# A Fourier stage's second step: table halves stand, data moves, and transposes turn the result

## The chip, the cores and the metric

The kernel runs on one NeuronCore of one Trainium2 chip. The metric is device microseconds for one execution of the whole program. Engines are named as in the profile: PE (TensorE products), PEld (its weight loads), DVE (VectorE), ACT (ScalarE), POOL (GpSimd), SP (SyncE, which issues nearly all DMA transfers here). Each engine takes its own instructions in order, and they meet through semaphores.

## The reference, cut to what matters

One encoder layer is applied to two sequences, a prompt of 256 rows and a sample of 2048 rows, each with 1024 features, in float32. The input projection gives six parts of 512 columns: q, k, v, a gate z_a, the Fourier input u, and a gate z_f. Neighbourhood attention uses q, k and v. The Fourier part is

```
ug   = u.reshape(b, s, 8, 64)                 # 8 groups of 64 features
spec = fft2(ug, axes=(sequence, feature), norm='ortho')
y_f  = spec.real.reshape(b, s, 512) @ w_f + b_f
```

and the two parts, each normalised and gated, go through an output product, a norm and a residual addition:

```
mixed = concat([rms_norm(y_a, g_na) * silu(z_a), rms_norm(y_f, g_f) * silu(z_f)])
out   = x + rms_norm(mixed @ w_out, g_post)
```

## The kernel before, in words

The program has three long parts on PE. The first 550 us or so hold the input projection (lines L160 to L162 under the tile name `mm`), with large products split into a high and a low float32r half and multiplied three times. In that part the first step of the sample's Fourier transform is made too (`u_stage1`), and its result goes to HBM as `ZD`. Then comes a short stage, the one that changes, and behind it the Fourier output `py` (`y_mm`, `y_out`), attention, and the output product.

The sequence transform of 2048 is made as 128 times 16. The first step has done the 128. What the second step reads is a tile per group of four frequencies: `zgs[gq][g]`, with 128 partitions (4 frequencies, real and imaginary, 16 positions) and 512 columns, which are the feature columns, folded so that the even and odd halves of a group of 64 can be used apart. `gq` runs over 0 to 3, `g` over 0 to 3. `d2` is the table of cosines and sines of the second step; for each group it has 128 partitions and 128 columns, 64 for the real part (A) and 64 for the imaginary part (B).

The old second step is `stage2(gq, zg, c)`, called for `c` from 0 to 4 in each `gq`. For `c` under 4 it takes 128 feature columns as the stationary operand and moves 64 columns of the table (the A half for c = 0 and 1, the B half for c = 2 and 3). The result has features on its 128 partitions, as the next step needs it. For `c` = 4 it takes the 64 columns that belong to feature 0 and feature 32 of each group, in pieces of 32. Each block of four `g` fills a PSUM tile `pab` of 256 columns, taken by turns from two buffers with tag "b" and one with tag "c". `split_ab` takes it out: a high half by a copy with rounding (ACT, or DVE for the first blocks), and a low half by a subtraction on DVE. The halves go to `AB` (c under 4) and `a32` (c = 4). With `gq` = 0 stand the products of one Nyquist column (`pny`), with `gq` = 2 those of the prompt's transform of 129 columns (`pup`), each in tiles of tag "a", of which there are three, and each block right behind the main block of the same `c`.

Behind `gq` = 1 and `gq` = 2, `pq(m)` multiplies the table of the feature transform with the matrix `w_f` (`wf`, 1 MB, loaded at the start of this stage) and splits the result into `PQ[m]`. Behind the last block `w32` is made from `nw`, two copies on ACT and one subtraction on DVE. They are placed behind the last instruction that `split_ps` put on its engine (`last[0]`).

Then `y_mm` multiplies `PQ` with `AB`, twelve products and one of `w32` with `a32`, into tiles of tags "a" and "b"; `y_out` adds a bias on ACT and combines on DVE (L1286, L1294). Two loads of a piece of the output weight, `wr`, are issued (L1257) when the memory of the stage before is free, and split on ACT and DVE (L1263, L1264) between the evacuations of `y_out`.

What sets the order: PE's order is that of the program everywhere. From the close of `man` (L972) until `order` (L1342) the order on ACT, DVE, POOL and SP is made by the framework's planner, which goes by program order and its own estimate of when operands are there. Before and behind that stretch it is written out by hand. In the stretch fall also the casts of the keys (`split_k`, L1096 on ACT, L1097 on POOL), which wait for a load of `kl`, and the issues of all loads for the start of attention.

`ptb` are two PSUM tiles of a whole bank, with tag "t". The projection's `mm` tiles used these buffers before; later attention uses them for transposes (`transp`) and others.

Of the kernel before, what the change touches and what calls it, by code (L numbers as in the profile page):

```python
# [10 lines left out]
F32 = mybir.dt.float32  # L11
# [153 lines left out]
def build(tc, A, O):  # L165
    nc = tc.nc
# [23 lines left out]
    ident = cst.tile([128, 128], F32, name="ident")  # L190
# [10 lines left out]
    dnyq = cst.tile([128, 3], F32, name="dnyq")  # L201
# [8 lines left out]
    ps = es.enter_context(tc.tile_pool(name="ps", bufs=3, space=PSUM))  # L210
# [545 lines left out]
    for b in range(16):  # L756
# [13 lines left out]
        if 2 <= b < 8:  # L770
            x, y = divmod(b, 2)
# [7 lines left out]
        p = mmt(512)[:, :TP]  # L779
# [54 lines left out]
    zgs = []  # L834
    for i in range(16):
# [29 lines left out]
        def src(a):  # L865
            if kind % 2 == 0:
                return a.rearrange("p (x c) -> p x c", c=32)
            if kind == 1:
                return a.rearrange("p (a j) -> p a j", j=256)
            return a.rearrange("p (x b c) -> p x b c", b=2, c=16)  # L870
# [13 lines left out]
        for j in range(7):  # L884
            for f, d in ((u_load, 0), (u_split, 4), (u_stage1, 6)):
                x = 7 * pr + j - 7 - d
# [31 lines left out]
            if sg == 0:  # L918
                x, y = divmod(7 * (pr - 1) + j, 14)
# [19 lines left out]
            if i == 15 and j in (1, 3, 4, 5):  # L939
                if j == 1:  # L940
                    d2 = [load_d(0), load_d(1)]
# [4 lines left out]
            p = mmt(512)  # L946
# [37 lines left out]
    sqs = sqp.tile([128, T], F32, name="sqs")  # L984
    ab = pf.enter_context(tc.tile_pool(name="ab", bufs=1))
    ptb = [ps.tile([128, 512], F32, tag="t", name="ptb", bufs=2) for i in range(2)]
    for x in ptb:
        nc.vector.memset(x, 0.0)
    pg = ExitStack()
    sm = pg.enter_context(tc.tile_pool(name="smF", bufs=1))  # L990
    cs2 = sm.tile([128, 2, 64], F32, name="cs2")
# [5 lines left out]
    f256 = sm.tile([128, 2, 258], F32, name="f256")  # L997
    nc.sync.dma_start(f256, A["f256"])
    up = sm.tile([128, 2, 512], F32, name="up")
# [17 lines left out]
    def dft(p, c, pairs):  # L1017
        sts = [(p[32 * r:32 * r + 32], slice(256, 512, 8)) for r in range(3)] if c == 4 else \
            [(p, slice(c * 128, c * 128 + 128))]
        for out, cols in sts:  # L1020
            for x, (z, d) in enumerate(pairs):
                nc.tensor.matmul(out, z[:, cols], d, start=x == 0, stop=x == len(pairs) - 1)  # L1022


    def split_ab(gq, c, view, p):
        if c < 4:
            split_ps(view(AC[c][0]), view(AC[c][1]), p, gq == 0 and c < 3)
        else:
            nc.scalar.copy(view(a32), p)
            lo = view(a32[64:96])  # L1030
            nc.vector.tensor_tensor(out=lo, in0=p[64:96], in1=lo.bitcast(F32), op=ALU.subtract)

    def stage2(gq, zg, c):
        m = int(c in (2, 3))
        np_ = 96 if c == 4 else 128
        x = (gq * 5 + c) % 3 == 2
        p = ps.tile([np_, 4, 64], F32, tag="c" if x else "b", name="pab", bufs=1 if x else 2)
        for g in range(4):
            dft(p[:, g, :], c, [(zg[g], d2[gq // 2][:, (gq % 2) * 4 + g, m * 64:m * 64 + 64])])
        split_ab(gq, c, lambda a: a[:, :1024].rearrange("p (k q g l) -> p q g k l", k=16, q=4, g=4)[:, gq],  # L1040
                 p.rearrange("p g (k l) -> p g k l", l=4))
        if gq == 0:
            p = ps.tile([np_, 1], F32, tag="a", name="pny")
            dft(p, c, [(zg[0], dnyq[:, m:m + 1])])
            split_ab(gq, c, lambda a: a[:, 1024:1025], p)
        if gq == 2:
            p = ps.tile([np_, 129], F32, tag="a", name="pup")
            dft(p, c, [(up[:, t], f256[:, t, 129 * m:129 * m + 129]) for t in range(2)])
            split_ab(gq, c, lambda a: a[:, 1025:1154], p)

    PQ = {}
    w32 = ab.tile([96, 512], F32R, name="w32")

    def pq(m):
        h = gt([128, 2, 512], F32R, "pqh")
        l = gt([128, 2, 512], F32R, "pql")
        for c in range(2):
            p = ps.tile([128, 512], F32, tag="a", name="ppq")
            for x in range(2):
                nc.tensor.matmul(p[64 * x:64 * x + 64], cs2[:, m, :], wf[:, 2 * c + x, :], start=True, stop=True)  # L1060
            if m == 0:
                split_ps(h[:, c], l[:, c], p)
                continue
            nq_ = sm.tile([128, 512], F32, name="nq", bufs=2)
            nc.scalar.copy(nq_, p)
            nc.gpsimd.dma_start(nw[16 * c:16 * c + 16:4], nq_[::32])
            nc.scalar.activation(h[:, c], p, AF.Copy, scale=dnyq[:, 2:3])
            nc.vector.scalar_tensor_tensor(out=l[:, c], in0=p, scalar=dnyq[:, 2:3], in1=h[:, c].bitcast(F32),
                                           op0=ALU.mult, op1=ALU.subtract)
        PQ[m] = h, l  # L1070

    for gq in range(4):
        for c in range(5):
            stage2(gq, zgs[gq], c)
        if gq in (1, 2):
            pq(2 - gq)
    with tc.issue_after(last[0].ins):
        for r in (0, 64):
            nc.scalar.copy(w32[r:r + 32], nw)
        nc.vector.tensor_tensor(out=w32[32:64], in0=nw, in1=w32[:32].bitcast(F32), op=ALU.subtract)  # L1080
# [161 lines left out]
    sm = pg.enter_context(tc.tile_pool(name="smY", bufs=2))  # L1242
    sqy = pq_.enter_context(tc.tile_pool(name="sqy", bufs=1, side="right"))
    y0 = sqy.tile([128, 4, TP], F32, name="y0")
    for t, (g, x) in enumerate(zip(G, (0, 640))):
        g["w"] = []
        for c0, w in g["t"]:
            n = 2 * g["nr"] * w
# [556 lines left out]
```

## Time and profile before

| | us |
|---|---|
| median of 3 runs | 966.51 |
| lowest, highest | 965.75, 966.55 |
| the profiled execution, whole | 965.94 |
| its span in the trace | 964.1 |
| PE busy | 955.2 |
| DVE busy | 703.4 |
| ACT busy | 496.7 |
| POOL busy | 427.0 |

In the profile, a row of a timeline gives start, length, engine, line, operation and shapes ("128*64 128x512" is a product with 64 stationary columns and 512 moved). The lengths of products overlap, since one enters the array while another leaves it. The time that a product costs PE is read from the distance between starts. Rows of waits say who waited for whom, how long in total, how many times, and the longest. The granted clock is full in all slices of this profile.

### The profile page before, as it was taken

To read this page: it belongs to the slowest core of one execution; us is meant where nothing else is said; L and a number is where in the kernel's file an instruction comes from. 1 tells how busy PE (TensorE), PEld (TensorE's weight loads), DVE (VectorE), ACT (ScalarE), POOL (GpSimd) and SP (SyncE) were. 2 spreads that over 40 slices of the span, in tenths; PEclk is the share of its full clock that TensorE was granted. 3 is DMA by queue.
4 is the path that set the end of the run, shared out by engine and by line. 5 is a ranking of instruction groups with operands and counts; after the bars stand their busy time and mean duration, and the time that the engine had idled before them with its cause. 6 is when DMAs were issued, how large, how long until landed. Compare 5 with 4: busy or idle time off the path is not lost.

```text
span 964.1 us, 16993 instructions
## 1 busy us (share of the span) xinstructions
PE 955.2 (99%) x5743; PEld 799.0 (83%) x5743; DVE 703.4 (73%) x1310; ACT 496.7 (52%) x1077; POOL 427.0 (44%) x400
## 2 busy tenths in 40 slices
PE   9999999999999999999999999999999999999997
PEld 7889988888888888888888889888788887888886
DVE  5768978787876855687877458776765656659997
ACT  5845676423334532233344267677666676644443
POOL 2200002464751202674665043577677686524544
PEclk9999999999999999999999999999999999999999
DMA  8899796557848883499888896598877998979993
GB/s 304 317 354 380 248 348 243 199 203 263 298 185 345 299 347 123 181 362 360 308 294 327 306 335 225 169 285 292 258 235 238 287 285 286 301 253 346 332 353 122
DMA packets 140942, 269.81 MB, mean 280 GB/s; under 512 B 13402, under 2 KB 81840, under 8 KB 137464
## 3 DMA queue, kind: packets, MB, share of 16 engines
q1 hardware_dynamic: 140360, 268.32, 79.8%
q8 instruction: 46, 0.75, 0.3%
q10 hardware_dynamic: 432, 0.39, 0.2%
q14 instruction: 40, 0.33, 0.1%
q0 software_dynamic: 64, 0.02, 0.0%
HBM read 179.00 MB, written 96.81 MB: 286 GB/s over the span
## 4 chain that ended last, share of the span: by engine, by line
PE 96%; DVE 1%; DMA 1%; issue 0%; ACT 0%; DVEq 0%; SPq 0%; ACTq 0%
PE po L1454 20%; PE mm L161 18%; PE mm L160 18%; PE mm L162 18%; PE pv L1543 6%; PE ptb L1527 6%; PE s L1185 4%; PE pab L1022 2%; DMA wr<-wo 1%; PE py L160 1%; DMA gpre<-gpre 0%; PE py L162 0%; PE py L161 0%; PE ppq L1060 0%; PE pz L162 0%
## 5 line engine op out<-in xcount | busy, mean ns | idle before, releaser
L160 PE MATMUL mm<-xh,wa 128*128 128x512 f32 x448 | 174.4, 389 | 0.0
L162 PE MATMUL mm<-xh,wa 128*128 128x512 f32 x448 | 174.3, 389 | 0.0
L161 PE MATMUL mm<-xl,wa 128*128 128x512 f32 x448 | 174.3, 389 | 0.0
L532 POOL TENSOR_TENSOR ws<-wr 128x512 f32<-128x512 f32 x16 | 23.7, 1480 | 221.0 <-DVE vuo L505 123.8
L1219 POOL TENSOR_SCALAR w<-w,m 128x465 f32<-128x465 f32 (+9 forms) x136 | 84.7, 635 | 43.5 <-DVE m L1216 34.0
L162 PEld LDWEIGHTS mm<-xh,wa 128*128 128x128 f32 x448 | 84.1, 188 | 17.6
L160 PEld LDWEIGHTS mm<-xh,wa 128*128 128x128 f32 x448 | 84.1, 188 | 17.6
L161 PEld LDWEIGHTS mm<-xl,wa 128*128 128x128 f32 x448 | 84.1, 188 | 17.4
L1454 PE MATMUL po<-wo,yh 128*128 128x512 f32 x272 | 90.5, 414 | 0.0
L547 DVE TENSOR_TENSOR wa<-wr,wa 128x512 fp32r<-128x512 f32 x60 | 72.8, 1222 | 21.8 <-ACT wa L546 21.3
L1454 PE MATMUL po<-w,yh 128*128 128x512 f32 x280 | 86.8, 391 | 0.0
L1212 ACT ACTIVATE w<-w,m 128x465 f32<-128x465 f32 (+9 forms) x136 | 78.3, 579 | 13.3 <-DVE m L1207 12.9
L1207 DVE CUSTOM_DVE_ANT_1 w<-s,tb 128x465 f32<-128x465 f32 (+8 forms) x124 | 61.2, 531 | 9.8 <-PE s L1185 9.3
L161 PE MATMUL mm<-vl,xh 128*128 128x512 f32 x168 | 65.5, 390 | 0.2 <-DVE vl L478 0.2
L162 PE MATMUL mm<-vh,xl 128*128 128x512 f32 x168 | 65.4, 389 | 0.0
L160 PE MATMUL mm<-vh,xh 128*128 128x512 f32 x168 | 65.4, 389 | 0.0
L585 POOL TENSOR_TENSOR mt<-mt,rmask 128x880 f32<-128x880 f32 (+2 forms) x24 | 50.3, 2110 | 32.2 <-DVE mt L581 25.9
L1454 PEld LDWEIGHTS po<-w,yh 128*128 128x128 f32 x280 | 52.2, 188 | 10.9 <-issue 0.4
L1531 DVE COPY pt<-ptb 120x384 f32<-120x384 f32 (+5 forms) x72 | 40.5, 563 | 27.6 <-PE ptb L1527 27.4
L873 DVE TENSOR_TENSOR f<-u,mm 128x512 f32<-128x512 f32 x64 | 43.5, 679 | 22.3 <-PE mm L162 13.6
L546 ACT CAST wa<-wr 128x512 fp32r<-128x512 f32 x60 | 36.5, 618 | 44.7 <-PE mm L162 18.2
L1527 PE MATMUL ptb<-ident,w 128*120 128x128 f32 (+8 forms) x422 | 58.9, 276 | 0.0
(265 smaller groups left out, 2387.4 us busy)
## 6 DMA issues: line engine op xcount, KB each, us to landing
wr<-wz SPq DMA_DIRECT2D x48, 512.0 KB
vl<-sD SPq DMA_DIRECT2D x20, 512.0 KB
xm<-xm SPq DMA_DIRECT2D x9, 1024.0 KB
oD<-ofs SPq DMA_DIRECT2D x18, 512.0 KB
of<-oD SPq DMA_DIRECT2D x18, 512.0 KB
yr<-yD SPq DMA_DIRECT2D x34, 256.0 KB
zD<-f SPq DMA_DIRECT2D x16, 512.0 KB
xD<-nx SPq DMA_DIRECT2D x14, 512.0 KB
```

The lines of the kernel that those rows point to most:

```text
L160: nc.tensor.matmul(out, lh, rh, start=first, stop=False)
L161: nc.tensor.matmul(out, lh, rl, start=False, stop=False)
L162: nc.tensor.matmul(out, ll, rh, start=False, stop=last)
L547: nc.vector.tensor_tensor(out=o[:, 1], in0=src, in1=o[:, 0].bitcast(F32), op=ALU.subtract)
L585: nc.gpsimd.tensor_tensor(out=o, in0=i, in1=rmask[:, m0:m0 + n].unsqueeze(2).to_broadcast([128, n, 80]), op=ALU.add)
L873: nc.vector.tensor_tensor(out=dst(f, b), in0=src(uu[u]), in1=src(p), op=op)
L1207: nc.vector.tensor_tensor_reduce(out=rows(g["w"][b][:, h, :n], w), in0=rows(g["s"][2 * b + h][:, :nr * sw(w)], sw(w))[:, :, :w], in1=tv, s ...
L1212: nc.scalar.activation(w, w, AF.Exp, bias=m[:, h:h + 1], scale=-1.0, accum_out=m[:, 2 + h:3 + h])
L1219: nc.gpsimd.tensor_scalar(w, w, m[:, 4 + h:5 + h], 1.0, ALU.mult, ALU.mult)
L1454: nc.tensor.matmul(p, (d["l"] if x == 2 else d["h"])[:, c], w(n, int(x == 1), c), start=j == 0, stop=j == 11)
L1527: nc.tensor.transpose(ptb[h][:nk, j * 128:j * 128 + 128], g["w"][b][:, h, c0:c0 + nk], ident)
L1543: nc.tensor.matmul(p[hs, b], g["v"][:nk, v, hs], g["pt"][b][:nk, h, j * 128:j * 128 + 128], start=j == 0, stop=j == len(ch) - 1)
```

## The change

In `stage2`'s place stand four functions.

`z_mm(gq)` makes the main products the other way round. The table's halves of 64 columns stand, and 256 columns of `z` move: the A half with columns 0 to 255, the B half with columns 256 to 511. For each `g` the two go to partitions 0 to 63 and 64 to 127 of the same 256 columns of `ptb`. Two `g` fill one of the two tiles, which is then copied to an SBUF tile `zt` of 512 columns, the first by DVE and the second by ACT. The result has frequencies on its partitions.

`z_turn(gq)` brings features back to the partitions: eight transposes of 128x128 from `zt` into two PSUM tiles of tag "b", each of 512 columns, which hold an A part and a B part for each `g`. Four calls of `split_ab` take them out, with 256 columns each as before.

`z_32(gq)` is the old block `c` = 4, always in the one tile of tag "c". `z_rest` makes the Nyquist column or the prompt's columns for all five `c` in a row, in tiles of tag "a".

In the new order, `z_turn` of one `gq` stands behind `z_mm` of the next, and the last `z_turn` stands at the end. The two memsets of `ptb` are gone.

```diff
-    for x in ptb:
-        nc.vector.memset(x, 0.0)
...
-    def stage2(gq, zg, c):
-        m = int(c in (2, 3))
-        np_ = 96 if c == 4 else 128
-        x = (gq * 5 + c) % 3 == 2
-        p = ps.tile([np_, 4, 64], F32, tag="c" if x else "b", name="pab", bufs=1 if x else 2)
...
+    def z_mm(gq):
+        for x in range(2):
+            for g in range(2 * x, 2 * x + 2):
+                for m in range(2):
+                    ms = slice(64 * m, 64 * m + 64)
+                    nc.tensor.matmul(ptb[x][ms, g % 2 * 256:g % 2 * 256 + 256], d2[gq // 2][:, gq % 2 * 4 + g, ms],
+                                     zgs[gq][g][:, 256 * m:256 * m + 256], start=True, stop=True)
+            zt[gq, x] = sm.tile([128, 512], F32, tag="zt", name="zt", bufs=4)
+            (nc.scalar.copy if x else nc.vector.tensor_copy)(zt[gq, x], ptb[x])
+
+    def zview(gq):
+        return lambda a: a[:, :1024].rearrange("p (k q g l) -> p q g k l", k=16, q=4, g=4)[:, gq]
+
+    def z_turn(gq):
+        for j in range(2):
+            p = ps.tile([128, 4, 128], F32, tag="b", name="pab", bufs=2)
+            for g in range(4):
+                j0 = g % 2 * 256 + j * 128
+                nc.tensor.transpose(p[:, g], zt[gq, g // 2][:, j0:j0 + 128], ident)
+            for m in range(2):
+                split_ab(gq, 2 * m + j, zview(gq), p[:, :, 64 * m:64 * m + 64].rearrange("p g (k l) -> p g k l", l=4))
+
+    def z_32(gq):
+        p = ps.tile([96, 4, 64], F32, tag="c", name="pab", bufs=1)
         for g in range(4):
...
+            dft(p[:, g, :], 4, [(zgs[gq][g], d2[gq // 2][:, gq % 2 * 4 + g, :64])])
+        split_ab(gq, 4, zview(gq), p.rearrange("p g (k l) -> p g k l", l=4))
+
+    def z_rest(gq, src, n, x0, x1):
+        for c in range(5):
+            m = int(c in (2, 3))
+            p = ps.tile([96 if c == 4 else 128, n], F32, tag="a", name="pz")
+            dft(p, c, src(m))
+            split_ab(gq, c, lambda a: a[:, x0:x1], p)
+
+    zt = {}
...
-    for gq in range(4):
-        for c in range(5):
-            stage2(gq, zgs[gq], c)
-        if gq in (1, 2):
+    z_mm(0)
+    z_rest(0, lambda m: [(zgs[0][0], dnyq[:, m:m + 1])], 1, 1024, 1025)
+    z_32(0)
+    for gq in range(1, 4):
+        z_mm(gq)
+        z_turn(gq - 1)
+        z_32(gq)
+        if gq == 2:
+            z_rest(gq, lambda m: [(up[:, t], f256[:, t, 129 * m:129 * m + 129]) for t in range(2)], 129, 1025, 1154)
+        if gq < 3:
             pq(2 - gq)
+    z_turn(3)
     with tc.issue_after(last[0].ins):
```

More of the change, by code (lines that the diff above doesn't have):

```diff
@@ L1031, in split_ab @@
             nc.vector.tensor_tensor(out=lo, in0=p[64:96], in1=lo.bitcast(F32), op=ALU.subtract)
-    def stage2(gq, zg, c):
-        m = int(c in (2, 3))
-        np_ = 96 if c == 4 else 128
-        x = (gq * 5 + c) % 3 == 2
-        p = ps.tile([np_, 4, 64], F32, tag="c" if x else "b", name="pab", bufs=1 if x else 2)
-        for g in range(4):
[L1039 to L1049, printed above, removed]
+    def z_mm(gq):
[7 more added lines that the diff above has]
+            (nc.scalar.copy if x else nc.vector.tensor_copy)(zt[gq, x], ptb[x])
```

## The prediction

> **What bounds the kernel now.** First the page, its busy shares and its chain of work.
>
> ```profile
> PE 955.2 (99%) x5743; PEld 799.0 (83%) x5743; DVE 703.4 (73%) x1310; ACT 496.7 (52%) x1077; POOL 427.0 (44%) x400
> ...
> PE 96%; DVE 1%; DMA 1%; issue 0%; ACT 0%; DVEq 0%; SPq 0%; ACTq 0%
> ```
>
> TensorE sets the time, so a product taken away is worth its length, but only if nothing else ends the stage. The change sits in one short stage, so next the timeline of PE there (start, length, line, form).
>
> ```profile
> 549.80 1.00 PE L1022 MATMUL pab<-d,zg 128*128 128x64 f32 x8
> 550.64 0.33 PE L1022 MATMUL pny<-dnyq,zg 128*128 128x1 f32 x2
> 550.83 1.08 PE L1022 MATMUL pab<-d,zg 128*128 128x64 f32 x8
> ...
> 554.25 0.72 PE L1022 MATMUL pab<-d,zg 128*32 128x64 f32 x24
> 554.80 0.24 PE L1022 MATMUL pny<-dnyq,zg 128*32 128x1 f32 x6
> 554.98 4.44 PE L1022 MATMUL pab<-d,zg 128*128 128x64 f32 x56
> 559.35 1.94 PE L1060 MATMUL ppq<-wf,cs 128*64 128x512 f32 x8
> 561.22 1.10 PE L1022 MATMUL pab<-d,zg 128*128 128x64 f32 x8
> ...
> 567.94 1.94 PE L1060 MATMUL ppq<-wf,cs 128*64 128x512 f32 x8
> 569.81 4.44 PE L1022 MATMUL pab<-d,zg 128*128 128x64 f32 x56
> 574.18 0.45 PE L160 MATMUL py<-abh,pqh 128*128 128x386 f32 x1
> 574.47 0.34 PE L161 MATMUL py<-abl,pqh 128*128 128x386 f32 x1
> ...
> 576.40 0.34 PE L1281 MATMUL py<-a,w 96*128 96x386 f32 x1
> ```
>
> The stage runs from 549.80 to 574.18, 24.4 us without a hole. Starts, not lengths, give prices, since products overlap. An f32 product is two instructions. Then the chain in order of time behind the stage, and the waits of PE from 548 to 605.
>
> ```profile
> 575.44 5.81 DMA wr<-wo
> 581.28 0.73 ACT wo L1263
> ...
> 586.39 1.01 DVE Y L1294 x6
> 587.54 0.41 PE py L160
> ```
>
> ```profile
> PE py L160 <- DVE Y L1294: 0.2, 1, 0.2
> ```
>
> That is the second bound. The load of `wr` cannot start until `w32` is made, its split on ACT and DVE stands ahead of Y's additions, and PE waits for these at 587.54. PE catches up with this chain already; if PE leaves the stage earlier and the chain doesn't, it waits longer there. Last, who holds the DMA queue (waits of SP from 530 to 600, then its timeline).
>
> ```profile
> SPq L1153 <- DMA kl<-kD: 1.9, 1, 1.9
> SPq L1257 <- DVE w L1080: 1.9, 1, 1.9
> ...
> SPq L1092 <- DMA wf<-wf: 1.1, 1, 1.1
> ```
>
> ```profile
> 556.98 1.91 SPq L1092 DMA_DIRECT2D kl<-kD  x2
> ...
> 567.03 0.33 SPq L1153 DMA_DIRECT2D v<-vD  x1
> ...
> 575.44 0.84 SPq L1257 DMA_DIRECT2D wr<-wo  x2
> ```
>
> The two L1092 issues span 556.98 to 558.89, and 1.1 us of that is a wait for `wf`. So `wf` lands at about 558.5, only 0.85 us before its first use at 559.35. In the same way `kl`'s second half lands at 567.0. The `wr` load waits 1.9 us for DVE's `w`, and for nothing of the queue's.
>
> **The change part by part.** Old prices: the four 128-column blocks of one `gq` cost 8 instructions each, 0.84 us (549.80 to 550.64). A plain `gq` with its 32-column block takes 4.37 (554.98 to 559.35); less 0.55 for that block (554.25 to 554.80), a block is 0.95. I take 0.89, the middle: 16 blocks, 14.2 us removed.
>
> New prices. For `z_mm` the trace has two near forms, both with 64 stationary columns: L1060 above, 8 in 1.87 us with 512 columns moved (0.234 each), and `pv` with 128 columns:
>
> ```profile
> 611.66 1.09 PE L1543 MATMUL pv<-pt,v 80*64 80x128 f32 x16
> 612.68 0.43 PE L1185 MATMUL s<-kh,qh 64*128 64x352 f32 x2
> 613.74 0.66 PE L1527 MATMUL ptb<-ident,kh 128*128 128x128 f32 x4
> 614.15 0.71 PE L1454 MATMUL po<-wo,yh 128*128 128x512 f32 x2
> ```
>
> That is 16 in 1.02, 0.064 each. 256 columns lie between 0.117 (half of 0.234) and 0.128 (twice 0.064); I take 0.117, 16 instructions, 1.87 us per `gq`. A transpose is one instruction: 4 in 0.41 us (613.74 to 614.15), so 8 take 0.82 per `gq`. Four times 2.69 is 10.8: PE's own work falls by 14.2 - 10.8 = 3.4 us (2.7 to 4.5 with the bounds above). `z_32`, the Nyquist column and the prompt's 129 columns keep their products and only move.
>
> The Trainium skill, "TensorE: Matmul & The Clock Gate", section "Why this matters for your kernels", says that narrow products (M under 128) whose outputs lie in different column groups run side by side, 2.38 times as fast for three. The two halves of `z_mm` are such a pair, and by that it would take 0.94 rather than 1.87. The trace disagrees: L1060's halves go to the same two column groups and take 0.234 each, one after another.
>
> Added on the other side: per `gq` two evacuations of 128x512, one on ACT and one on DVE. ACT's price is L1065's 0.58; DVE's is at most 0.69, the longest of L1531. The 16 splits of 256 columns stay, with a stride in PSUM: price unchanged, that of the rows below. Two memsets go from DVE; nobody waited for them, so they are worth nothing.
>
> ```profile
> L1531 DVE COPY pt<-ptb x72: 416/557/692, 608.0 to 858.2; 120x384 f32<-120x384 f32 x24, 120x512 f32<-120x512 f32 x16, 80x256 f32<-80x256 f32 x8, 96x384 f32<-96x384 f32 x8
> ```
>
> ```profile
> 551.80 1.28 ACT L974 ACT_TABLE_LOAD   x1
> ...
> 560.48 0.58 ACT L1065 COPY nq<-ppq 128x512 f32<-128x512 f32 x1 [0.62 <-PE ppq L1060]
> ...
> 565.70 0.68 ACT L1096 CAST kh<-kl 128x576 fp32r<-128x576 f32 x1
> ...
> 567.88 0.67 ACT L1096 CAST kh<-kl 128x576 fp32r<-128x576 f32 x1
> ...
> 573.63 0.37 ACT L1014 CAST abh<-pab 128x256 fp32r<-128x256 f32 x1 [0.22 <-PE pab L1022]
> 573.90 0.61 ACT L1079 CAST w<-nw 32x512 fp32r<-32x512 f32 x1
> ...
> 574.80 0.62 ACT L1079 CAST w<-nw 32x512 fp32r<-32x512 f32 x1
> ```
>
> ```profile
> 574.03 0.42 DVE L1015 TENSOR_TENSOR abl<-pab,abh 128x256 fp32r<-128x256 f32 x1 [0.47 <-ACT abh L1014]
> 574.54 0.68 DVE L1080 TENSOR_TENSOR w<-nw,w 32x512 fp32r<-32x512 f32 x1
> ```
>
> Starts on these engines lie some 0.1 us closer than the lengths: 0.27 for ACT's half of a split (573.63 to 573.90), and, by the same reduction, 0.32 for DVE's.
>
> *Stretch one, to the first `pq`.* From 549.80: `z_mm(0)` 1.87, Nyquist 4 x 0.19 + 0.18 = 0.94, `z_32` 0.55, `z_mm(1)` 1.87, `z_turn(0)` 0.82, `z_32` 0.55: sum 6.6, so PE is at `pq(1)` at 556.4, 2.95 us ahead. ACT's first evacuation can only start behind the table load (551.80 to 553.08); `z_mm(1)` overwrites that half at about 554.1, so this is covered. But `pq(1)` reads `wf`, which lands at 558.5; its place in the DMA queue doesn't change. PE stops for 2.1 us and starts `pq(1)` at about 558.6. Kept: 0.75.
>
> *Stretch two, to the end of `pq(0)`.* From `pq(1)`'s end to `pq(0)` the old kernel takes 6.72 (561.22 to 567.94). Four blocks at 0.84 give way to 2.69: 0.67 less. The five prompt pieces (6.72 less four blocks and 0.55, so 2.8 or 0.56 each) now stand in a row and share three PSUM buffers, behind `z_turn(1)`'s four splits on ACT and DVE: between 0 and 0.5 us is given back; I take 0.1, since a piece takes PE longer than it takes either of the other two. `pq(0)` then ends at 558.6 + 1.87 + 6.05 + 0.1 + 1.87 = 568.5 instead of 569.81: 1.3 ahead.
>
> *Stretch three, the last `gq`.* `z_mm(3)` 1.87 to 570.4, `z_turn(2)` 0.82 to 571.2, `z_32` 0.55 to 571.7. Then `z_turn(3)` needs the two "b" buffers of `z_turn(2)`, and each is free only when both its splits are done. The first is full at 570.8; allow 0.25 us from PE to ACT (an estimate), then two halves on ACT and two on DVE behind them: both splits end at about 572.2, those of the second at about 572.9. `z_turn(3)` runs 572.25 to 572.65 and 572.95 to 573.35. The old order had blocks of work between these points; the new one has only `z_32`.
>
> *Stretch four, the tail.* Now nothing of the last `gq` has been split when PE is done. The first Y product needs block 0's high half (ACT, about 573.3); its second the low half (0.45 later), and block 1, in the second buffer and third in line, comes about 0.4 us late again. Two stalls near 0.4 and twelve products at 0.175 (574.47 to 576.40 is eleven) put the `w32` product at about 576.2, against 576.40. So PE ends level, some 0.2 ahead: the 3.4 us are gone, 2.1 to `wf`, the rest to buffers and the tail.
>
> *The chain.* `w32` comes behind the last split, which now leaves ACT at about 574.3 with the 32-column split and a `split_q` cast among them. Two copies later it is 575.4 to 576.1; before, 575.42 (574.80 + 0.62). The `wr` load moves by 0 to +0.7; I take +0.4, and as PE waits at this chain's end, PE does too.
>
> **Sum:** +0.4 us. The profiled execution took 965.94 us around a span of 964.1; the median of the runs is 966.51, 0.57 above it. The forecast stands on the median: 966.9. The likeliest case's own range is -0.8 (the buffers of stretch three free in time) to +1.4 (`wf` at 559.3, and up to 0.5 more in stretch two), 965.7 to 967.9. A change under 0.2%, 1.9 us, cannot be told from none with this kernel.
>
> **The rivals.**
>
> *Slower: ACT's queue is blocked by `kl` (0.33).* The order on ACT in this stage is the planner's, and fixed. The four L1096 casts read `kl`, whose second half lands at 567.0. Before, the third cast ran at 567.88, 0.85 after the landing. PE is now 0.75 to 1.3 ahead of its old place against DMA; a cast that keeps its distance from its own DMA stands among later splits, but one planned in front of the prompt's splits, the first of them ready at about 564.3 (560.5 + 1.87 + 0.82 + 0.55 + 0.56), holds all of them until 567.0. PE then stalls at the fourth piece (three buffers), from 565.4 to about 568: 2.5 us, less what it was ahead at the end (0.2), and `w32` moves as far. Price +2.0 to +3.5, 969.2 as its middle. It decides if the third cast comes before the prompt's second split. For it: ACT is fuller, four copies of 0.58 more. Against it: before, ACT waited at no cast.
>
> *Faster: PE's gain is kept (0.07).* `wf` lands before 557 and the last splits fall behind other work: -2 to -3.4, 963.8. Against it: the SP wait for `wf`, and the `wr` chain, which has no part that gets shorter. With it goes the case that the halves of `z_mm` run side by side (0.02): 0.94 less in each of the two `gq` behind the `wf` gate, 965.0 at best, and less where the tail bounds. The Trainium skill's rule on column groups, in the page named above, would give this; L1060's rows speak against it.
>
> *It does nothing for PE (part of the likeliest).* If `z_mm` costs 0.128 or more per instruction, 0.2 us more per `gq`; up to `pq(1)` the wait for `wf` takes it up, behind it 0.4 is lost: 967.3, still no change.
>
> **How the numbers follow.** Likeliest 0.58, blocked ACT 0.33, gain kept 0.09 with the side-by-side case. Faster by over 0.2% has 0.07, that is the kept gain without the side-by-side case, which ends at 965.0, within 0.2%. Slower has 0.33, within 0.60. The range leaves out most of the kept gain and the worst of the blocked case: 965.2 to 969.8.
>
> **What the profile after would show.** `z_mm` with 16 instructions in 1.87 us and 8 transposes in 0.82; PE idle in front of the `ppq` products from 556.4 to 558.6, put down to DMA `wf`; a short idle before `z_turn(3)` and before the first Y products, put down to the splits; the `wr` load issued within 0.7 us of 575.44. Wrong if PE starts `pq(1)` before 558, if ACT sits idle for `kl` with splits behind, or if the tail takes less than 0.3 us of stalls.

## The result, and the profile after

The changed kernel takes 972.20 us in the median (969.97 to 975.48, six runs) against 966.24 for the kernel before beside it: a ratio of 1.0064, with a 95% interval of 1.0046 to 1.0082. A second comparison of the same pair gave 969.81 against 966.03, 1.0047 (1.0032 to 1.0062). The change is slower by about half a per cent. The forecast was 966.9, with a range from 965.2 to 969.8.

The profiled execution took 969.97 us with a span of 968.1, 4.0 longer than before's 964.1. First the busy shares and the chain of work of its page.

```profile
PE 954.5 (99%) x5711; PEld 792.4 (82%) x5711; DVE 704.8 (73%) x1312; ACT 498.3 (51%) x1081; POOL 429.2 (44%) x400
...
PE 94%; DMA 3%; DVE 1%; SPq 1%; issue 0%; ACT 0%; DVEq 0%; POOL 0%; ACTq 0%; POOLq 0%
```

PE has 32 instructions less and almost the same busy time. PE's share of the chain fell from 96% to 94%, but that is not the stage: 4 us are 0.4% of the span, and in a second trace of the same program the share is 96% again, with 1% of DMA. What DMA has more here are transfers in the attention, shown below. What the stage lost is seen in the timeline of PE there (start, length, line, form, and in brackets the idle time ahead of a row and who ended it):

```profile
549.54 1.95 PE L1036 MATMUL ptb<-zg,d 128*64 128x256 f32 x16
551.42 0.83 PE L1020 MATMUL pz<-dnyq,zg 128*128 128x1 f32 x6
552.57 0.61 PE L1020 MATMUL pz<-dnyq,zg 128*128 128x1 f32 x8 [0.32 <-DVE abl L1013]
553.02 0.71 PE L1020 MATMUL pab<-d,zg 128*32 128x64 f32 x24
553.66 1.95 PE L1036 MATMUL ptb<-zg,d 128*64 128x256 f32 x16
555.54 1.09 PE L1049 MATMUL pab<-ident,zt 128*128 128x128 f32 x8
556.56 0.73 PE L1020 MATMUL pab<-d,zg 128*32 128x64 f32 x24
557.90 1.94 PE L1076 MATMUL ppq<-wf,cs 128*64 128x512 f32 x8 [0.61 <-DMA wf<-wf]
...
562.52 0.73 PE L1020 MATMUL pab<-d,zg 128*32 128x64 f32 x24
563.18 1.60 PE L1020 MATMUL pz<-f,up 128*128 128x129 f32 x12
566.90 1.90 PE L1020 MATMUL pz<-f,up 128*128 128x129 f32 x16 [2.12 <-DVE abl L1013]
568.74 2.91 PE L1076 MATMUL ppq<-wf,cs 128*64 128x512 f32 x8
571.48 1.89 PE L1036 MATMUL ptb<-zg,d 128*64 128x256 f32 x16
...
575.88 0.63 PE L1049 MATMUL pab<-ident,zt 128*128 128x128 f32 x4 [0.83 <-DVE abl L1013]
576.79 0.63 PE L1049 MATMUL pab<-ident,zt 128*128 128x128 f32 x4 [0.28 <-DVE abl L1013]
577.17 0.42 PE L160 MATMUL py<-abh,pqh 128*128 128x386 f32 x1
...
580.07 0.41 PE L1304 MATMUL py<-a,w 96*128 96x386 f32 x1
```

The measure used from here on is the **length of the stage**, from the start of its first product to the start of the first product of `w32`: 576.40 - 549.80 = 26.60 us before, 580.07 - 549.54 = 30.53 now. The stage is 3.9 us longer, and five waits of PE with 4.16 us in sum stand in it where there was none. The longest stands at the fourth piece of the prompt: three pieces (the twelve instructions of 563.18) fill the three "a" buffers, and the fourth waits 2.12 us for DVE's low half. Who keeps DVE waiting is seen on ACT (its timeline at that place).

```profile
562.19 0.81 ACT L1012 CAST abh<-pab 128x256 fp32r<-128x256 f32 x2
564.34 0.67 ACT L1119 CAST kh<-kl 128x576 fp32r<-128x576 f32 x1 [1.34 <-DMA kl<-kD]
564.92 0.64 ACT L1012 CAST abh<-pab 128x256 fp32r<-128x256 f32 x2
...
565.71 0.44 ACT L1012 CAST abh<-pz 128x129 fp32r<-128x129 f32 x2
566.03 0.69 ACT L1119 CAST kh<-kl 128x576 fp32r<-128x576 f32 x1
566.60 0.29 ACT L1012 CAST abh<-pz 128x129 fp32r<-128x129 f32 x1
566.76 1.27 ACT L1119 CAST kh<-kl 128x576 fp32r<-128x576 f32 x2
```

The first cast of `kl` stands in the middle of the four splits of `z_turn(1)`. It waits 1.34 us for its transfer, the first half of `kl`, and with it everything behind it on ACT: two splits, the 32-column split, and the pieces' splits, the first of which comes at 565.71 although PE had made the pieces from 563.18 on.

The stop has a second price. The stretches behind it (PE busy, then the granted clock):

```profile
567.00:568.00 1.00, 1.00 (x10) 0.66 0.93 360
568.00:569.00 1.00, 1.00 (x14) 0.50 1.12 306
569.00:570.00 1.00, 1.00 (x4) 0.50 1.07 259
570.00:571.00 1.00, 1.00 (x4) 0.63 0.29 75
571.00:572.00 1.00, 1.00 (x10) 1.00 0.65 145
```

From about 567.3 to 570.7 PE runs at half its clock: the eight instructions of `pq(0)` take 571.48 - 568.74 = 2.74 us instead of the 1.87 of before. The forty slices of the page show 9 everywhere and hide this; only short stretches show it.

Behind the stage, the second product of the attention tells where the shift goes. Its first group, the group at 807 us and the last one, in the kernel before (the first stands in the prediction, at 611.66) and then in the changed one:

```profile
807.42 0.77 PE L1543 MATMUL pv<-pt,v 128*64 128x128 f32 x10
...
859.49 1.54 PE L1543 MATMUL pv<-pt,v 128*64 128x128 f32 x24
```

```profile
614.67 0.55 PE L1566 MATMUL pv<-pt,v 80*64 80x128 f32 x6
...
810.44 0.77 PE L1566 MATMUL pv<-pt,v 128*64 128x128 f32 x10
...
863.47 0.77 PE L1566 MATMUL pv<-pt,v 128*64 128x128 f32 x10
```

The shift is +3.01 at 611, still +3.02 at 807, and +3.98 at 859. So the 4.0 us are: stage begun 0.26 earlier, +3.93 in the stage, -0.66 between the stage and the attention (the 0.2 wait for Y's additions is gone, since PE itself comes later), and +0.97 between 807 and 822 us. That last part did not come again in a second trace of the same program, which the next section has. The chain of work has two transfers there, in order of time:

```profile
802.33 8.05 DMA v<-vD
...
814.61 4.42 DMA ql<-qD
```

### The profile page after: what moved, and what is told of

Its sections match the earlier page's. It is cut to its first block, busy times and chain, and to the rows that moved or that the text cites. A ratio compares the mean times of both kernels' runs of the same rounds, so it can differ in the third digit from the quotient of the medians.

```text
span 968.1 us, 16945 instructions
## 1 busy us (share of the span) xinstructions
PE 954.5 (99%) x5711; PEld 792.4 (82%) x5711; DVE 704.8 (73%) x1312; ACT 498.3 (51%) x1081; POOL 429.2 (44%) x400
## 4 chain that ended last, share of the span: by engine, by line
PE 94%; DMA 3%; DVE 1%; SPq 1%; issue 0%; ACT 0%; DVEq 0%; POOL 0%; ACTq 0%; POOLq 0%
PE po L1477 19%; PE mm L161 18%; PE mm L162 18%; PE mm L160 18%; PE ptb L1550 5%; PE pv L1566 5%; PE s L1208 4%; PE py L160 1%; PE py L161 1%; PE py L162 1%; DMA v<-vD 1%; DMA kl<-kD 1%; DMA ql<-qD 0%; DMA gpre<-gpre 0%; SPq L1176 0%
## 5 line engine op out<-in xcount | busy, mean ns | idle before, releaser
L547 DVE TENSOR_TENSOR wa<-wr,wa 128x512 fp32r<-128x512 f32 x60 | 68.7, 1154 | 22.8 <-ACT wa L546 22.5
```

The source lines that it names most:

```text
L547: nc.vector.tensor_tensor(out=o[:, 1], in0=src, in1=o[:, 0].bitcast(F32), op=ALU.subtract)
```

## The experiments

Two theories stood against each other behind the result. **A**: ACT's order, with a cast of `kl` ahead of the splits, makes the loss, through the stop and the slow clock behind it. **B**: the new transform itself is the loss (its waits for buffers, `wf` and the tail). The runs up to the kernel with `pq(1)` later take these apart; those behind it look for what was left.

### The changed kernel once more

> The changed kernel once more, unaltered, for its spread and a second trace. Every theory expects 970 to 975 us. In this trace, too, PE should stop about 2.1 us in front of the fourth prompt piece. The runs differ by more than 5 us, which the stage itself does not explain: what lies above +4 us should be found behind the stage (in the first trace one attention step lost 0.97 us to a late load).

969.81 us, 1.0047 (1.0032 to 1.0062). The stage takes 30.55 us (30.53 in the first trace): the same stop (1.89 us at the fourth piece), the same half clock, the same waits at the end. In this trace the attention lost nothing between 807 and 859 us (a shift of +3.14 at 611, +2.96 at 859). So the stage's length repeats, and the loss at 807 to 822 us does not.

### The casts of `kl` behind `pq(0)`

```diff
+            pq_last = last[0]
...
-    for x in range(4):
-        split_k(KK[0], x)
+    with tc.issue_after(pq_last.ins):
+        for x in range(4):
+            split_k(KK[0], x)
```

> The changed kernel with one constraint of order: the four casts of the keys stand on ACT behind the splits of pq(0). Theory A (ACT's order: the first cast holds z_turn(1)'s splits back until kl lands): the 2.1 us stop in front of the fourth prompt piece goes, and with it the slow clock behind it (1.6 us: the fourth and fifth piece at 1.84 instead of 1.12, pq(0) at 2.74 instead of 1.87), so 3 to 4 us less than the changed kernel: about 968.5. Theory B (the two-buffer wait of z_turn(3) and the tail are what costs): less than 1 us less, 971 or more.

The four casts stand on ACT behind the splits of `pq(0)`. 967.69 us, 1.0020 (1.0008 to 1.0032): 2.1 us below the changed kernel beside it, less than the 3 to 4 that theory A expected and more than the 1 that B allowed. The timeline of PE and the stretches, from the places of the stop on:

```profile
565.38 1.33 PE L1020 MATMUL pz<-f,up 128*128 128x129 f32 x16 [0.26 <-DVE abl L1013]
566.63 1.94 PE L1076 MATMUL ppq<-wf,cs 128*64 128x512 f32 x8
568.40 1.90 PE L1036 MATMUL ptb<-zg,d 128*64 128x256 f32 x16
...
573.40 1.06 PE L1049 MATMUL pab<-ident,zt 128*128 128x128 f32 x8 [1.42 <-DVE abl L1013]
```

```profile
565.00:570.00 5.00, 4.74 (x42) 1.00 1.05 347
570.00:575.00 5.00, 3.53 (x46) 1.00 0.67 188
```

The 2.12 us at the fourth piece are 0.26, the clock is full throughout, and `pq(0)` takes 1.77 us. The stage takes 27.9 us, 2.6 less than the changed kernel's (27.6 and 3.0 less in a second trace, further down). Theory A holds for these 2.6 to 3.0. What is left, 1.3 above before, stands in waits: 0.95 for `wf`, and 1.42 ahead of `z_turn(3)` in place of 0.83 and 0.28. Three of the casts now stand ahead of the copy of the last `zt` on ACT, but they don't explain the 1.42: a later kernel with no cast there waits 1.38 and 0.28.

### A filler in the stop

Eight products (sixteen instructions) that nobody reads are put ahead of the fourth piece, so that PE works through the stop; ACT's order stays.

```diff
+            if gq == 2 and c == 3:
+                for y in range(8):
+                    h = slice(64 * (y % 2), 64 * (y % 2) + 64)
+                    nc.tensor.matmul(ptb[1][h, :256], d2[1][:, 3, h], zgs[2][3][:, 256 * (y % 2):256 * (y % 2) + 256],
+                                     start=True, stop=True)
```

> The changed kernel with eight extra products (z_mm(2)'s last group repeated, 1.87 us, results unused) in front of the fourth prompt piece, where PE stands idle 2.12 us anyway. If the half clock behind that stop comes from the idle time, the clock stays at 1.0, pq(0) takes 1.87 instead of 2.74, and the kernel gets 1 to 1.6 us faster than the changed one although PE does more. If the clock has another cause, the time stays within 0.3 us of the changed kernel or rises.

967.87 us, 1.0025 (1.0015 to 1.0035): 1.9 us less than the changed kernel, with more work on PE.

```profile
564.66 1.95 PE L1066 MATMUL ptb<-zg,d 128*64 128x256 f32 x16
566.61 1.33 PE L1020 MATMUL pz<-f,up 128*128 128x129 f32 x16
567.86 1.94 PE L1081 MATMUL ppq<-wf,cs 128*64 128x512 f32 x8
```

```profile
565.00:570.00 5.00, 5.00 (x44) 1.00 1.03 323
```

The pieces go on at 566.61, as late as in the changed kernel (566.90 and 566.66). What is won in the stage is the clock: it takes 29.4 us, 1.15 less than the 30.55 of the changed kernel beside it. The sixteen instructions and `pq(0)` behind the stop are 1.7 us faster than there (3.02 from 566.61 to 569.63, against 4.71 from 566.66 to 571.37); 0.46 of that is given back at `z_turn(3)`, where the first wait grows from 0.83 to 1.29. So the slow clock is an effect of PE standing still, not of the late splits themselves, and is a cost of its own beside the stop.

### The last `gq` the old way

With the casts moved as above, the last `gq` is made by the old blocks, so that the tail has its old form: `z_old(3)`, the four blocks of the old `stage2`, in the place of `z_mm(3)` and `z_turn(3)`.

```diff
-        z_mm(gq)
+        if gq < 3:
+            z_mm(gq)
         z_turn(gq - 1)
+        if gq == 3:
+            z_old(3)
...
-    z_turn(3)
```

> e1 with the last gq made the old way (four blocks of 128 standing columns, no z_mm(3) and z_turn(3)). If buffers and tail cost what the prediction's stretches three and four say (0.4 + 0.4 + about 0.8 us of stops, less the 0.7 us that the new form saves on PE), it is 0.7 to 1.5 us faster than e1: about 967.3. If the tail is hidden by the chain of w32 and wr, it equals e1 within 0.3 us.

973.80 us, 1.0075 (1.0063 to 1.0087): slower than all others. The stage takes 33.35 us. The old blocks stand behind `z_turn(2)`, in the same two buffers, and its splits stand behind two of the casts on ACT; PE stops for 2.22 us ahead of them, and the half clock then lasts through the tail. This run does not tell what the old tail is worth, since a new stop covers it.

### Casts behind the last copy of `w32`

```diff
-            nc.scalar.copy(w32[r:r + 32], nw)
+            w32_last = nc.scalar.copy(w32[r:r + 32], nw)
...
+    with tc.issue_after(w32_last.ins):
```

> The changed kernel with the four casts of the keys behind the last copy of w32, so that none stands among the stage's splits. This is the case that the prediction took for the likeliest (splits in program order). If its stretches three and four are right, PE waits about 0.8 us in two pieces before z_turn(3), the w32 product comes at about 576.2 to 576.6, and the time lies 0 to 1 us above the kernel before. If more of the loss lies elsewhere, it stays near e1 (1.7 us above).

969.17 us, 1.0037 (1.0025 to 1.0049). The stage takes 27.7 us with the waits that the likeliest case of the prediction named: 0.62 for `wf`, 0.32 at the Nyquist column, 0.26 at the prompt's pieces, 1.38 and 0.28 at `z_turn(3)`. This is close to the order on ACT for which 966.9 was forecast (there the casts were to stand among later splits), and it still loses 1.1 us in the stage. Behind the stage the four casts now hold up the first evacuation of `y_out`: in the trace's chain of work, ACT's casts of 576.81 to 579.21 stand ahead of it. From the `w32` product to the attention it takes 35.9 us, and 34.7 to 35.3 in the three traces of before.

### `z_turn(3)` in the three-buffer tag

The kernel above, and the last turn's two tiles come from tag "a", where none of `z_turn(2)`'s splits has to be done first.

```diff
-            p = ps.tile([128, 4, 128], F32, tag="b", name="pab", bufs=2)
+            t = "a" if gq == 3 else "b"
+            p = ps.tile([128, 4, 128], F32, tag=t, name="pab", bufs=3 if gq == 3 else 2)
```

> e6 with z_turn(3) in PSUM tiles of tag a (three buffers) instead of b (two). If the two-buffer wait costs, PE's waits before z_turn(3) go, and the kernel gains 0.4 to 0.8 us on e6. If the splits on ACT and DVE are the bound there, the wait moves behind z_turn(3) to the first Y products, and the time stays within 0.3 us of e6.

968.24 us, 1.0019 (1.0006 to 1.0031). PE no longer waits at `z_turn(3)`; instead the first Y products wait 0.65 for ACT's high half and 0.45 for DVE's low half. The stage takes 26.9 us, 0.75 less. Of the 1.66 us that the buffers cost, 1.1 come back as the wait that stood behind them.

### The prompt part later

The kernel above, with `pq(1)` behind `z_32(2)` rather than behind `z_32(1)`, so that `wf` has time to land.

```diff
+            pq(1)
             z_rest(gq, lambda m: [(up[:, t], f256[:, t, 129 * m:129 * m + 129]) for t in range(2)], 129, 1025, 1154)
-        if gq < 3:
-            pq(2 - gq)
+        if gq == 2:
+            pq(0)
```

> e7 with pq(1) moved behind z_32(2), so that wf has landed when PE reaches it. The 0.6 to 1.0 us wait for wf goes. If the PE saving then reaches the end, the time falls by 0.7 to 1 us against e7, to or below the kernel before. If the chain of w32 and the wr load ends the stage anyway, it falls by less than 0.3 us.

968.56 us, 1.0022 (1.0011 to 1.0033). The wait for `wf` is gone; the pieces now wait 0.56 and 0.35 for the splits of `pq(1)`, whose buffers they take over. The stage takes 26.5 us, as long as before's 26.6, and the traced execution took 966.01 us with a span of 964.1, before's own. But the median did not follow: it is 2.6 us above before's, and not below the 968.24 of the kernel ahead.

### The last `gq` the old way, in that kernel

> e8 with the last gq made the old way, so that blocks of work again stand between the last splits. The new form saves about 0.7 us of PE in a gq, the tail was priced at 0.8 to 1.2 us. Tail theory: 0.2 to 0.8 us faster than e8 and faster than the kernel before by 0.5 to 2 us. If a stop of 2 us or more arises before the first old block (the two b buffers of z_turn(2)), the half clock comes back and it is 2 us or more slower than e8.

The edit is that of the earlier run with old blocks, made in the kernel with `pq(1)` later. 970.49 us, 1.0058 (1.0043 to 1.0073). The old blocks stop again, and here is what follows such a stop when the work behind it is long (PE's timeline, then its stretches):

```profile
571.67 6.96 PE L1020 MATMUL pab<-d,zg 128*128 128x64 f32 x56 [1.63 <-issue]
```

```profile
572.00:576.00 4.00, 4.00 (x25) 0.61 0.87 273
576.00:580.00 4.00, 4.00 (x36) 0.50 0.43 149
580.00:584.00 4.00, 4.00 (x16) 0.61 0.89 287
```

The old blocks and `z_32`, 56 instructions, take 6.96 us where the kernel before took 4.44. The 1.63 us of idle, for which the profile shows no releaser, were followed by 10.2 us at half the clock.

### What the rest is not: two controls

The variants with a short stage still measured some 0.2% above before. Two controls: the kernel before against itself, and the kernel before with nothing but the casts moved behind `w32` (the edit shown above).

> The kernel before, unchanged, entered as if it were a change. What is asked: how large a difference the comparison shows with no change at all, and whether a second execution of it shows late loads in the attention. Both theories of the remaining 2 us expect a ratio of 1.000 with 0.1% on either side. If the remainder is a matter of single executions (DMA transfers of the attention that come late between 805 and 830 us in some of them, whatever the kernel), this trace too should lose 0 to 1 us there against the first trace of before. If it belongs to the changed stage, the starts of the second product of the attention agree with the first trace within 0.3 us at both ends.

> The kernel before with one line of the variants: the casts of kl are issued behind the last copy into w32. If the remainder of 2 us (about 0.2%) that all variants with moved casts share comes from the casts' place, this kernel has it too: 1.002. If it belongs to the changed transform, this kernel stays at 1.000 with 0.1% on either side. In its trace the wf wait and the four-product groups of the transform are those of before, and the w32 product starts at 576.4 with 0.3 on either side.

The unchanged kernel gave 965.56 us, 0.9997 (0.9989 to 1.0006), the one with moved casts 966.62, 1.0004 (0.9995 to 1.0013). So the comparison has no offset, and the casts' place accounts for no more than about 0.1%. Both stages take 26.59 us, to 0.01 the same as the first trace. The attention is not that steady: from the first to the last group of its second product the shift against the first trace goes from -0.45 to +0.86 in the one, from -0.09 to +1.19 in the other, with a wait of 0.76 and of 0.38 for DVE's `dt`.

The two variants again, for a second trace:

> The variant with moved casts, the last turn in the three-buffer tag and the prompt part later, once more, for a second trace: its first had the span of before (964.1), its median was 2 us above. If the remainder lies in the stage, this trace shows it there: the second product of the attention starts 1 to 3 us later than before's from the first group on. If it lies in the attention's loads, the first groups start within 0.3 us of before's and the shift comes between 805 and 840 us. Ratio 1.002 with 0.1% on either side in both cases.

> The changed kernel with the casts of kl behind the first inverse part, once more: its first trace was 0.4 us late at the start of the attention and 2.8 us at its end. If the loss between 805 and 840 us is a matter of single executions, it has another size this time (0 to 2.5) while the 0.4 at the start stays within 0.3; if it goes with this kernel, it is 2.4 again with 0.3 on either side. Ratio 1.002 with 0.1% on either side.

968.15 us, 1.0016 (1.0007 to 1.0025), and 967.68, 1.0018 (1.0009 to 1.0027). The stage of the first is 26.50 (26.51 the first time), that of the second 27.56 (27.93). The second's loss in the attention, 2.4 us in its first trace, is -0.2 in this one. That first trace has transfers in its chain at the place where the changed kernel's first had them: 7.38 us of `za` from 802.14 and 4.44 of `ql` from 813.45.

### The short stage with no cast held

The kernel with `pq(1)` later, and the casts where the planner puts them; in this program the first of them stands behind the high halves of four of the five pieces.

> The variant with the last turn in the three-buffer tag and the prompt part later, but with no instruction held back: the casts of kl go where the planner puts them, which in this program is behind the splits of the prompt pieces. If the moved casts cost 0.4 to 0.8 us behind the stage (the kernel before with moved casts had 0.4 in its median and one wait of 0.2 to 0.6 for the Y adds more in its trace), this one is 0.4 to 0.8 below the variant with casts behind w32 (968.2 to 968.6): 967.4 to 968.1, and the first product of w32 comes within 0.3 us of 26.5 behind the start of the stage. If the changed stage is worth a gain once nothing waits, it is below before: 965.4 to 966.0. If ACT's order still stops PE at the prompt pieces, the trace shows a wait of over 1.5 us there and the granted clock at one half behind it, and the time is 969 or more.

967.67 us, 1.0017 (1.0006 to 1.0027). No stop, a full clock, a stage of 26.51 us. That is where the theory of the held casts put it (967.4 to 968.1), but the distance to the kernel with held casts is inside both intervals, and the control says the same: about 0.1% at most. It did not fall below before. Three more traces of it, and one of the kernel before, show where a longer execution loses its time.

> The variant with no held casts once more, for a trace alone: its first trace was 0.6 us behind before's at the end while the median of its twelve runs was 1.4 us behind. If the rest lies in the transfers of the attention, an execution that is 1 us or more slower than before's 964.1 us of span shows the loss between 805 and 840 us and starts the attention's second product within 0.3 us of 61.5 us behind the start of the stage, as the first trace (61.45). If it lies in the stage, that distance is longer by 1 us or more.

> As the run before it: the distance from the stage's start to the first group of the attention's second product is 61.5 us with 0.3 on either side and a slow execution loses its time between 805 and 840 us, or the distance itself is longer.

> As the two runs before it: the distance from the stage's start to the first group of the attention's second product is 61.5 us with 0.3 on either side and a slow execution loses its time between 805 and 840 us, or the distance itself is longer.

> The kernel before, unchanged, for a third trace: its first two lost 0 and 1.3 us between 805 and 840 us against each other. If late transfers there hit this kernel as often as the variants, this trace shows a loss of 0.5 us or more there in about every second look; the stage takes 26.6 us from its start to the product of w32 as in both traces.

They took 966.55, 967.51 and 968.42 us, and the kernel before 965.76. The stage is 26.51 us in all four traces of the variant, from the shortest to the longest, and 26.60, 26.59 and 26.59 in the three of before. The longest execution is the one that tells most (first product of the stage, product of `w32`, three groups of the attention's second product):

```profile
550.78 1.95 PE L1036 MATMUL ptb<-zg,d 128*64 128x256 f32 x16
...
577.29 0.42 PE L1306 MATMUL py<-a,w 96*128 96x386 f32 x1
...
612.72 0.55 PE L1568 MATMUL pv<-pt,v 80*64 80x128 f32 x6
...
808.48 0.77 PE L1568 MATMUL pv<-pt,v 128*64 128x128 f32 x10
...
861.93 0.88 PE L1568 MATMUL pv<-pt,v 128*64 128x128 f32 x12
```

Against the first trace of before it begins the stage 0.98 late, is 1.06 late at 611 and 807 us, and 2.44 late at 859. Its chain has `za` and `ql` there again (6.70 and 4.36 us). The other two lost 0.2 and 1.6 us behind the first of these groups, and between stage and attention they had one wait of 0.9 and one of 0.65 for Y's additions.

From the start of the stage to the attention these three traces take 62.58, 62.31 and 61.94 us, not the 61.5 with 0.3 on either side that was expected; before takes 61.86, 61.32 and 61.68. As the stage itself is level, the time lies behind it: from the `w32` product to the attention the six traces with a stage of 26.5 us take 35.7 on average, before's three 35.0. So about 0.7 of the rest stands there, of which 0.4 are PE's waits for Y's additions. Before with moved casts took 35.8 there as well, so it does not need the new transform.

So the rest does not lie in the length of the stage. A part lies right behind the stage, and a part in the attention; that either comes from the change is not shown. Transfers stand in the chain between 800 and 842 us in 6 of the 15 traces of the changed kernel and its variants, and in none of the four of before and of before with moved casts. That fits a rest of 1 to 2 us in the median, but 0 of 4 is too few to show that before is spared, and before lost 1.3 us in the attention in one of its traces without them. The order of the transfers on their queue is the same in the changed kernel and before, up to the output product. Why they would come late more often behind the new stage stays open; so does whether they do.

## Why the prediction was wrong

**The wait of ACT** is the step that failed. The likeliest case let PE stop only for `wf`, for the buffers of `z_turn(3)` and in the tail; a cast "that keeps its distance from its own DMA stands among later splits", so no split of the prompt's stretch was to wait for a transfer. In the planner's order the first cast of `kl` stands between the second and the third split of `z_turn(1)`. ACT stood 1.34 us there for the first half of `kl`, PE stopped for 2.12 us (1.89 in the second trace), and the clock was at one half for 3.4 us behind it. With the casts moved, and nothing else, the stage was 2.6 to 3.0 us shorter.

The rival with 0.33 had the kind of loss right: splits held by a cast of `kl`, PE stopped at the fourth piece, from 564.8 (told: 565.4) to 566.9 (568). It had the wrong cast. Its mark was the third cast, which reads the second half of `kl`, ahead of the prompt's second split; the third cast came at 566.76, behind the prompt's third split, so by that mark the rival would not have come at all. The prediction never asked when the first half of `kl` lands. That the stop lasted nearly as long as told is therefore in part luck. The argument against the rival, that before "ACT waited at no cast", said nothing of an order that the planner makes anew for another program. Two of the signs that the prediction named for being wrong did come: ACT idle for `kl` with splits behind, and `pq(1)` before 558, at 557.90.

**The rival's price** was 2.5 us of stop, less 0.2 for the head start. Measured were stops of 2.12 and 1.89 us, and with them 1.6 to 1.7 us of half clock. In the first trace `pq(0)` took 2.74 us instead of 1.77, and the sixteen instructions from 566.90 took 1.84 instead of 1.25; in the second, `pq(0)` took 3.46. (The shorter figures are those of the run with the casts behind `pq(0)`.) No term of the prediction had a clock in it, although its likeliest case, too, had a stop of 2.1 us. The rival's 2.3 and these 1.6 make 3.9, which is what the stage measured, but the fit is chance: the stop was 0.4 to 0.6 shorter than told, and without the stop the stage is not 0.2 us shorter than before, as told, but 1.0 to 1.3 longer.

**Stretch one** was right in kind, wrong in size. PE waits for `wf`, but 0.58 to 0.95 us and not 2.1: PE came at 557.3 rather than 556.4, and `wf` had landed at 557.9 rather than 558.5. The first step was later than summed because the products cost more than the rows of other places said. `z_mm` is right to the hundredth (1.88, told 1.87), so its two halves do not run side by side. But eight transposes take 1.02, not 0.82; `z_32` takes 0.66 in the new order, not 0.55; the Nyquist column 1.28, not 0.94, and a wait of 0.32 for DVE stands in it that the sum did not have.

**The saving of 3.4 us** is thereby smaller: 4 x 0.2 + 4 x 0.1 + 0.3 = 1.5 less. (Its lower bound of 2.7 left out the prediction's own dearer price of 0.128 for an instruction of `z_mm`; with it the bound is 2.0.) The kernel with no cast held confirms the smaller saving. Its timeline of PE, first product of the stage and first Y product:

```profile
550.14 1.95 PE L1036 MATMUL ptb<-zg,d 128*64 128x256 f32 x16
...
573.71 0.45 PE L160 MATMUL py<-abh,pqh 128*128 128x386 f32 x1
```

These are 23.57 us, less waits of 1.23 is 22.3, against 24.4 before. That is 2.0 us saved.

**Stretches three and four, and the sum.** `z_turn(3)`'s two waits (told some 0.55 and 0.3) measured 0.83 and 0.28, and 1.38 and 0.28 where no stop stands ahead. The tail's stalls before the `w32` product, told as two of 0.4, came as one of 0.43 and some 0.3 of slower starts in the kernel with no cast held, and as 0.7 of slower starts in the changed one. For the order that was held likeliest the prediction has the `w32` product 0.2 us earlier than before. The run closest to it, with the casts behind `w32`, has the stage 1.1 us longer, and 969.17 for the whole; a part of that is the casts' own hold on `y_out`. The run with the casts behind `pq(0)` gave 967.69. These are 3.2 and 1.7 us above the kernel before beside them, where the likeliest case said +0.4 and its range ended at +1.4. So the likeliest case would have missed as well. Its central statement stands: a saving on PE that is at once eaten by buffers, `wf` and the tail. When the waits were taken away one by one, the stage came to 26.5 us, level with 26.6.

**The chain of `wr`**, on which alone the sum's +0.4 stood, was no cost in the changed kernel. The load was issued at 580.05, 4.6 us later than before and far beyond the 0.7 that was told, and PE still had no wait for Y's additions in that trace: PE itself was later. Where the stage is short, the additions do make PE wait, 0.6 to 0.9 us in four of six traces, which supports the prediction's view of a second bound just behind PE.

## What to carry to other kernels

Where a planner orders an engine's queue, an instruction that waits for a transfer can be placed in front of work that PE needs next; look for each such instruction in the stretch, find what stands behind it, and hold it behind that work. A stop of PE of about 2 us is to be priced with what follows it: the stop here was 2 us, and the slow clock behind it another 1.2 to 1.7, more where the work behind was long. Counting products says little in a stage that is as long as its buffers, its loads and its tail let it be: 2 us of PE's work were saved, and in the best order found they only paid for the waits.

## What was not expected of the hardware

After stops of 2.12 and 1.89 us in this stage (the two traces of the changed kernel) the granted clock was one half for 3.4 us each; after stops of 2.22 and 1.63 (the two kernels with old blocks), for 10.2 us each, three times as long. It fell between 0 and 1.3 us behind the end of the stop. After stops of 1.42, 1.38 and 1.29 us it stayed at 1.00. The Trainium skill, "TensorE: Matmul & The Clock Gate", section "Why this matters for your kernels", asks for no idle gaps of PE above about 3 us. Taken as the limit, that rule would have let all of these stops pass; the trace disagrees, and 1.6 us was enough here. The runs do not tell whether the length of the stop decides or what PE did ahead of it: shorter waits of 0.3 to 0.8 us stand ahead of each.

The length of the stage, from its first product to the first of `w32`, repeats to 0.02 us over traces of the same program (26.59 to 26.60, 26.50 to 26.51, 30.53 to 30.55). The exception is the kernel with casts behind `pq(0)` (27.93 and 27.56, with waits for `wf` of 0.95 and 0.58). Whole executions of one program spread over some 2 to 6 us. A trace is thus a far sharper measure of one stage than the time of the whole.
